# Three slots more between the first layer norm's sums and its mean, and one weight unit's low part moved to VectorE

## The chip, the cores and the metric

The kernel runs on one core of a Trainium2 chip. The metric is the device time of one launch in microseconds (us); lower is better. The engines are PE (TensorE, matrix products), ACT (ScalarE), DVE (VectorE), POOL (GpSimd) and SP (SyncE, which only issues DMAs). Each engine works through its own instruction queue in order.

## The reference, cut to what matters

Two layers of a trunk over 256 latent and 256 context tokens with 1024 channels. In each layer an input projection feeds a convolution branch, an attention branch and sigmoid gates:

```
u = a * sigmoid(g); u = dwconv1d(u, dw, dw_b)          # 31 taps, 512 channels
u = silu(layernorm(u, ln_g, ln_b))                     # mean and variance over the 512 channels
y_conv = u @ w_conv_out
y_attn = merge_heads(neighbourhood_attention(...)) @ w_na_out
x = x + g1 * ((sigmoid(gate0) * y_conv + sigmoid(gate1) * y_attn) @ w_out)
```

A gated feed-forward network follows. The modulation vectors (shift, scale and gate of each norm) are products of a conditioning vector with a 1024 x 6144 matrix per layer.

## The kernel before, in words

Every weight product is made of three: a weight tile is split into a high part and a low part, and so is the activation, and `mm3` issues high x high (L187), weight high x activation low (L188) and weight low x activation high (L189). Weights come in units of 128 x 1024 (512 KB), each loaded by SP into one of four buffers `raw`. ACT rounds a unit to its high part `whi` (four buffers). The low part `wlo` (four buffers) is made in one of two ways. `wunit` has DVE subtract: `whi` by L168 on ACT, `wlo` by L169 on DVE. `wadded` is for the units listed in `ADDED`: ACT makes `whi` by L206, then its negative by L207 into `wlo`, and POOL issues a DMA that adds `raw` onto it (L208). A `raw` buffer is free for the next unit only when L169 has read it or the L208 transfer has landed; a `whi` buffer only when the last product that reads it is done.

Work that is not a weight product runs as generators in a list `side`. `slot()` advances each generator to its next `yield`. `group` calls it twice in each 24 products of a 512-wide gate tile, and once more often where a group has only 12 products (the branch projections). So the slots pace the side work against PE.

Two generators matter here. `ada_dots` makes the modulation vectors: it loads a unit of `w_ada` (buffers `own`) and DVE takes its dot product with one or two vectors (L293, two instructions of 128 x 1024 a unit, each followed by a short read of the accumulator). `layer_norm` first finishes the convolution taps (L659), then adds the four channel tiles (L940 to L942 into `ss`), and has PE multiply the sum by ones, which takes the mean over channels and copies it to all partitions (L945, into the PSUM bank `po`). DVE subtracts it (L948), ACT squares (L333, L340), DVE adds the squares (L344), some slots later PE sums them over channels (L358), DVE and POOL take the root (L366, L368), PE spreads it (L374), and L956 to L960 scale, apply swish and split the result into `sh` and `sl`.

The place is the first layer's gate tiles: U_IN+14+n is the unit of gate n. After the gates comes the attention branch's projection (units U_NA to U_NA+3, 8 groups of 12 products, read `oh` and `ol`; DVE multiplies each group with its gate by L983), then `finish(ln)`, then the convolution branch's projection (units U_CO on, reads `sh`, `sl`).

Program order alone does not set an engine's queue: the tile framework schedules the recorded instructions, so a shift of a generator by a slot reorders neighbours on several engines.

Of the kernel before, what the change touches and what calls it, by code (L numbers as in the profile page):

```python
# [43 lines left out]

U_GLU0, U_V, U_IN, U_NA, U_CO, U_WO, U_UP, U_DN = 0, 2, 6, 36, 40, 44, 52, 96
NU = 118
ADDED = {*((0, U_IN + i) for i in (*range(19), 20, 22, 24, 26, 28)), *((0, u) for u in (U_NA + 1, U_NA + 3, *range(U_CO, U_CO + 4))), *((1, U_IN + i) for i in (7, 8, 9, 14, 15, 16, 17))}
T_GLU, T_Q, T_K, T_GATE = 0, 6, 10, 14

SWAP16 = [(i + 16) % 32 for i in range(32)]  # L50
# [3 lines left out]
def trunk(ctx: ExitStack, tc: tile.TileContext, xt, cvec, crow, wall, wada, params, bias_t, rope_t, out):  # L54
# [13 lines left out]
    def nm(s):  # L68
        uid[0] += 1
        return f"{s}_{uid[0]}"  # L70
# [3 lines left out]
    def psum(tag="main"):  # L74
        return psp.tile([P, 512], F32, tag=tag, bufs=BANKS[tag], name=nm(tag))

    def tmp(w=512):
        return tp.tile([P, w], F32, tag="t", bufs=5, name=nm("t"))
# [68 lines left out]
    def pr(l, off, n):  # L147
        return par[:, l * NPAR + off : l * NPAR + off + n]
# [29 lines left out]
    def wunit(l, u, at=None, cuts=1):  # L178
        w, more = wparts(l, u, at, cuts)
        more()  # L180
        return w

    def cols(w, i):
        return sl(w[0], i), sl(w[1], i)
# [16 lines left out]
    def wadded(l, u):  # L201

        r = raw_unit(wall[l, u])
        hi = wp.tile([P, UW], F32R, tag="whi", bufs=4, name=nm("whi"))
        lo = wp.tile([P, UW], F32R, tag="wlo", bufs=4, name=nm("wlo"))
        act.copy(hi, r)  # L206
        act.mul(lo, hi.bitcast(F32), -1.0)  # L207
        pool.dma_start(lo, r, accum_op=ALU.add)  # L208
        return hi, lo

    def unit8(l, u, at=None):
        w = wadded(l, u) if (l, u) in ADDED else wunit(l, u, at)
        return [cols(w, i) for i in range(KD)]
# [133 lines left out]
    def sum_squares(n, T, apart=False):  # L347

        at = tp.tile([P, 512], F32, tag="ss", name=nm("ss"))
        return [SumSq(T, at[:, i * T : (i + 1) * T], apart) for i in range(n)]  # L350

    def rstd(ss, n, bank, rest=0):

        nt = ss.T // P
        pt = psum("pt")
        for i, p in enumerate(ss.parts):
            for t in range(nt):
                pe.matmul(  # L358
                    pt[:, t : t + 1], sl(p, t), one, start=i == 0 and t == 0, stop=i == len(ss.parts) - 1,
                    skip_group_check=True,  # L360
                )
        return (yield from root(pt, nt, n, bank, rest))
# [255 lines left out]
    for l in range(DEPTH):  # L618
        last = l == DEPTH - 1
# [4 lines left out]
        with ExitStack() if last else start as e1a:  # L624
# [21 lines left out]
            def conv_tap(j, t):  # L646
                if after[0] is not None:
                    with tc.issue_after(after[0].ins):
                        tap(j, t)
                else:  # L650
                    tap(j, t)
# [264 lines left out]
            with ExitStack() as e1c:  # L916
# [12 lines left out]
                def layer_norm():  # L929

                    while taps:
                        for _ in range(6 if last else 5):
                            if taps:
                                conv_tap(*taps.pop(0))
                        yield
                    pace[0] = 1.0 if last else 1.1
                    flat = [c.rearrange("p s t -> p (s t)") for c in cb]
                    sm = tp.tile([P, 512], F32, tag="ss", name=nm("ss"))
                    eng = pool if last else dve
                    eng.tensor_tensor(sm[:, :T], flat[0], flat[1], ALU.add)  # L940
                    eng.tensor_tensor(sm[:, :T], sm[:, :T], flat[2], ALU.add)
                    dve.tensor_tensor(sm[:, :T], sm[:, :T], flat[3], ALU.add)  # L942
                    yield
                    pm = psum("po")
                    pe.matmul(pm[:, :T], one.to_broadcast([P, P]), sm[:, :T], start=True, stop=True)  # L945
                    (s2,) = sum_squares(1, T)
                    for j in range(KC):
                        dve.scalar_tensor_tensor(flat[j], pm[:, :T], -1.0 / CONV, flat[j], ALU.mult, ALU.add)  # L948
                        s2.add(flat[j], j == KC - 1)
                    for _ in range(2 if last else 5):  # L950
                        yield
                    pb = yield from rstd(s2, CONV, "po", 0 if last else 2)
                    for j in range(KC):
                        sg = tmp()
                        g, b = pr(l, LNG + j, 1), pr(l, LNB + j, 1)
                        dve.scalar_tensor_tensor(flat[j], flat[j], g, pb[:, :T], ALU.mult, ALU.mult)  # L956
                        act.activation(sg[:, :T], flat[j], AF.Sigmoid, bias=b)
                        dve.scalar_tensor_tensor(flat[j], flat[j], b, sg[:, :T], ALU.add, ALU.mult)
                        act.copy(sh_[j], flat[j])
                        dve.tensor_tensor(sl_[j], flat[j], sh_[j].bitcast(F32), ALU.subtract)  # L960
                        yield
                    if last:
                        pace[0] = 0.4

                side.remove(conv)
                ln = layer_norm()
                add_side(ln)
                for n in range(n, 2 * KD):
# [5 lines left out]
                def branch(base, xh, xl):  # L974
                    for n in range(0, KD, 2):
                        w = (wadded if (l, base + n // 2) in ADDED else wunit)(l, base + n // 2)
                        for i in range(2):
# [68 lines left out]
        with ExitStack() as e2:  # L1046
# [45 lines left out]
            if last:  # L1092
# [14 lines left out]
                for i, ps in enumerate(pss):  # L1107
                    b = small([P, 1], "wb", 4)
                    act.copy(b, ps[:, S : S + 1])
                    u = ef.tile([P, S], F32, name=f"u{l}_{i}")  # L1110
# [221 lines left out]
```

## Time and profile before

| | |
|---|---|
| median of 3 runs | 1118.74 us (1118.72 to 1119.91) |
| the profiled execution's own time | 1120.4 us |
| its span, first to last instruction | 1118.6 us |
| PE busy | 1097.3 us, 98% of the span |
| DVE busy | 897.0 us, 80% |
| ACT busy | 591.1 us, 53% |
| POOL busy | 45.9 us, 4% |
| mean granted TensorE clock | 0.995 of full speed |

PE is busy nearly all the time, so a change is worth what it does to the few gaps in PE's row; an idle gap on another engine counts only if PE waits for what comes after it. The views used are the page, the waits (who waited for whom), the timeline (instructions in order of time with start, duration, engine, line, tile and in brackets the idle time before it) and the windows (busy time and granted clock in chosen stretches).

### The profile page before, as it was taken

The numbers are of one execution on the slowest core, as the hardware profiler recorded it, in microseconds if no ns is written. First come the engines' busy times: TensorE is split into PE (matmuls) and PEld (weight loads), VectorE is DVE, ScalarE is ACT, GpSimd is POOL, SyncE is SP. The second block draws the span as 40 slices with busy tenths as digits, with TensorE's granted clock in tenths as the row PEclk, the third lists the DMA queues.
The fourth block names the chain that finished last, engine by engine and source line by source line (L and its number), as shares of the span: only waits on it lengthen the run. The fifth ranks groups of instructions, "written<-read, shape, count | busy, mean of one in ns | idle before, by whom it ended". The sixth has DMA issues, their size and how long they took to land.

```text
span 1118.6 us, 18099 instructions
## 1 busy us (share of the span) xinstructions
PE 1097.3 (98%) x6900; PEld 952.0 (85%) x6900; DVE 897.0 (80%) x1634; ACT 591.1 (53%) x974; POOL 45.9 (4%) x61
## 2 busy tenths in 40 slices
PE   8999999899999999999999999999999999999997
PEld 7677777678889988888888888989889999999997
DVE  5568898889898788888888555789799888988773
ACT  4458878445333543434343223544877657666642
POOL 1011110010000000000000000000100000000000
PEclk9999999999999999999999999999999999999999
DMA  9978663967953354554557656557863574665781
GB/s 362 288 198 223 154 165 86 280 184 217 284 164 94 112 153 151 169 170 150 170 170 215 219 186 190 181 196 196 226 187 138 151 259 156 191 196 179 222 268 57
DMA packets 60806, 211.35 MB, mean 189 GB/s; under 512 B 7344, under 2 KB 7600, under 8 KB 60720
## 3 DMA queue, kind: packets, MB, share of 16 engines
q1 hardware_dynamic: 55104, 190.77, 53.1%
q0 software_dynamic: 5328, 19.40, 9.1%
q8 instruction: 54, 0.88, 0.3%
q14 instruction: 32, 0.26, 0.1%
q10 hardware_dynamic: 288, 0.04, 0.0%
HBM read 187.63 MB, written 1.05 MB: 169 GB/s over the span
## 4 chain that ended last, share of the span: by engine, by line
PE 77%; issue 7%; DVE 6%; ACT 5%; DMA 3%; SPq 1%; POOL 0%; POOLq 0%; DVEq 0%; ACTq 0%
PE main L187 23%; PE main L189 23%; PE main L188 23%; PE main L729 4%; DVE cb L659 3%; SPq L721 1%; DMA raw<-in_wall 1%; DMA sb<-in_crow 1%; PE sc L189 1%; PE sc L188 1%; DMA wlo<-raw 1%; PE sc L187 1%; ACT whi L206 1%; ACT wlo L207 1%; DVE wlo L169 1%
## 5 line engine op out<-in xcount | busy, mean ns | idle before, releaser
L187 PE MATMUL main<-h,whi 128*128 128x256 f32 (+1 forms) x1328 | 446.8, 337 | 0.0
L189 PE MATMUL main<-h,wlo 128*128 128x256 f32 (+1 forms) x1328 | 444.0, 336 | 2.6 <-DMA wlo<-raw 1.6
L188 PE MATMUL main<-h,whi 128*128 128x256 f32 (+1 forms) x1328 | 442.6, 334 | 0.1
L168 ACT CAST whi<-raw 128x1024 fp32r<-128x1024 f32 (+1 forms) x207 | 213.9, 1037 | 235.9 <-DMA raw<-in_wall 115.5
L169 DVE TENSOR_TENSOR wlo<-raw,whi 128x1024 fp32r<-128x1024 f32 (+1 forms) x207 | 248.3, 1206 | 91.2 <-ACT whi L168 90.3
L189 PEld LDWEIGHTS main<-h,wlo 128*128 128x128 f32 x1328 | 249.7, 189 | 32.1 <-DMA wlo<-raw 1.8
L187 PEld LDWEIGHTS main<-h,whi 128*128 128x128 f32 x1328 | 249.7, 188 | 30.7 <-issue 2.2
L188 PEld LDWEIGHTS main<-h,whi 128*128 128x128 f32 x1328 | 250.1, 189 | 28.4 <-DVE h L390 0.5
L659 DVE SCALAR_TENSOR_TENSOR cb<-u,par,cb 128x512 f32<-128x512 f32 (+1 forms) x240 | 144.3, 616 | 3.0
L187 PE MATMUL main<-fh,whi 128*128 128x256 f32 (+1 forms) x386 | 123.0, 319 | 0.0
L188 PE MATMUL main<-fl,whi 128*128 128x256 f32 (+1 forms) x386 | 122.9, 318 | 0.0
L189 PE MATMUL main<-fh,wlo 128*128 128x256 f32 (+1 forms) x386 | 122.9, 318 | 0.0
L293 DVE CUSTOM_DVE_ANT_0 t<-raw,sb,par 128x1024 bf16<-128x1024 f32 x72 | 91.5, 1278 | 0.0
L189 PEld LDWEIGHTS main<-fh,wlo 128*128 128x128 f32 x386 | 72.7, 188 | 5.6
L188 PEld LDWEIGHTS main<-fl,whi 128*128 128x128 f32 x386 | 72.7, 188 | 5.6
L187 PEld LDWEIGHTS main<-fh,whi 128*128 128x128 f32 x386 | 72.7, 188 | 5.5
L1059 ACT ACTIVATE t<-main,par 128x512 f32<-128x512 f32 (+1 forms) x82 | 50.7, 669 | 39.2 <-PE main L189 39.2
L206 ACT CAST whi<-raw 128x1024 fp32r<-128x1024 f32 x37 | 38.9, 1052 | 47.2 <-PE main L188 24.5
L293 DVE CUSTOM_DVE_ANT_0 t<-own,sb,par 128x1024 bf16<-128x1024 f32 x48 | 60.1, 1279 | 3.9 <-ACT g L704 3.9
L1060 DVE SCALAR_TENSOR_TENSOR t<-main,par,t 128x510 f32<-128x510 f32 (+1 forms) x82 | 47.6, 615 | 10.6 <-ACT t L1059 10.3
L1063 DVE SCALAR_TENSOR_TENSOR t<-main,par,t 128x510 f32<-128x510 f32 (+1 forms) x82 | 46.6, 610 | 0.0
L389 ACT ACTIVATE h<-t,mod 128x256 fp32r<-128x256 f32 x56 | 25.5, 502 | 37.8 <-DVE t L388 37.8
(222 smaller groups left out, 1295.1 us busy)
## 6 DMA issues: line engine op xcount, KB each, us to landing
raw<-in_wall SPq DMA_DIRECT2D x239, 512.0 KB, 4.4
raw<-in_wada SPq DMA_DIRECT2D x64, 512.0 KB, 4.5
wlo<-raw POOLq DMA_DIRECT2D x37, 512.0 KB, 6.2
own<-in_wada SPq DMA_DIRECT2D x24, 512.0 KB, 4.9
bias<-in_bias_t SPq DMA_DIRECT2D x8, 520.0 KB, 5.0
row<-in_wada SPq DMA_DIRECT2D x8, 512.0 KB, 4.8
sb<-in_crow SPq DMA_DIRECT2D x5, 512.0 KB, 5.9
x<-in_xt SPq DMA_DIRECT2D x8, 256.0 KB, 4.4
```

The lines of the kernel that those rows point to most:

```text
L168: act.copy(hi[:, c], r[:, c])
L169: dve.tensor_tensor(lo[:, c], r[:, c], hi[:, c].bitcast(F32), ALU.subtract)
L187: pe.matmul(ps, w[0], xh, start=start, stop=False)
L188: pe.matmul(ps, w[0], xl, start=False, stop=False)
L189: pe.matmul(ps, w[1], xh, start=False, stop=stop)
L206: act.copy(hi, r)
L293: dve.tensor_tensor_reduce(tmp().bitcast(BF16), r, v, 1.0, pr(l, BADA + n, 1), ALU.mult, ALU.add, mods[l][:, n, s : s + 1])
L659: dve.scalar_tensor_tensor(cb[j], src, w, cb[j], ALU.mult, ALU.add)
L729: mm = pe.matmul(pv[t], h1[n == 1][k][:, c], w[n == 2][:, b], start=k + n == 0, stop=k == KD - 1 and n == 2)
L1059: act.activation(c, pv_, AF.Identity, bias=pr(l, FDB + t, 1), scale=w[1])
L1060: dve.scalar_tensor_tensor(c[:, :, 1:], pv_[:, :, : S - 1], w[0], c[:, :, 1:], ALU.mult, ALU.add)
L1063: dve.scalar_tensor_tensor(c[:, :, : S - 1], pv_[:, :, 1:], w[2], c[:, :, : S - 1], ALU.mult, ALU.add)
```

## The change

In the first layer, `layer_norm` yields four times instead of once between the last addition into `ss` (L942) and the product that takes the mean, so that this product and all that follows it in the generator is recorded three slots later. In the second layer the unit U_IN+17, the weights of gate 3, leaves `ADDED`: its low part comes from a subtraction on DVE (L169) and no longer from ACT's L207 and POOL's accumulating DMA L208. All lines after L943 have a number greater by one in the changed kernel.

```diff
-ADDED = {..., *((1, U_IN + i) for i in (7, 8, 9, 14, 15, 16, 17))}
+ADDED = {..., *((1, U_IN + i) for i in (7, 8, 9, 14, 15, 16))}
 ...
                     dve.tensor_tensor(sm[:, :T], sm[:, :T], flat[3], ALU.add)
-                    yield
+                    for _ in range(1 if last else 4):
+                        yield
                     pm = psum("po")
                     pe.matmul(pm[:, :T], one.to_broadcast([P, P]), sm[:, :T], start=True, stop=True)
```

Three places show how the queues move. In the rows a name's number says which buffer's use it is.

On DVE, in the first layer, from the dot products on the unit own_2197 to the sum `ss` and the mean's subtraction. Before:

```order
L293 ISA t_2293,mod_108<-own_2197,sb_2165,par 128x1024
L293 ISA mod_108 128x1
L659 SCALAR_TENSOR_TENSOR cb_3_202<-u_3_215,par,cb_3_202 128x512
L169 TENSOR_TENSOR wlo_2375<-raw_2373,whi_2374 128x1024
L659 SCALAR_TENSOR_TENSOR cb_3_202<-u_3_215,par,cb_3_202 128x512 x3
L169 TENSOR_TENSOR wlo_2469<-raw_2467,whi_2468 128x1024
L659 SCALAR_TENSOR_TENSOR cb_3_202<-u_3_215,par,cb_3_202 128x512 x3
L942 TENSOR_TENSOR ss_2297<-ss_2297,cb_3_202 128x512
```

And now, from the low part wlo_2358 on:

```order
L169 TENSOR_TENSOR wlo_2358<-raw_2356,whi_2357 128x1024
L659 SCALAR_TENSOR_TENSOR cb_3_202<-u_3_215,par,cb_3_202 128x512
L293 ISA t_2374,mod_108<-own_2295,sb_2162,par 128x1024
L293 ISA mod_108 128x1
L659 SCALAR_TENSOR_TENSOR cb_3_202<-u_3_215,par,cb_3_202 128x512
L293 ISA t_2376,mod_108<-own_2295,sb_2165,par 128x1024
L293 ISA mod_108 128x1
L659 SCALAR_TENSOR_TENSOR cb_3_202<-u_3_215,par,cb_3_202 128x512
L169 TENSOR_TENSOR wlo_2460<-raw_2458,whi_2459 128x1024
L659 SCALAR_TENSOR_TENSOR cb_3_202<-u_3_215,par,cb_3_202 128x512
L942 TENSOR_TENSOR ss_2297<-ss_2297,cb_3_202 128x512
```

Between the tap after own_2197 and these rows the changed queue also has the two dots of own_2247, each with a tap behind it. So four dots that stood behind L942 now stand ahead of it, and two of them ahead of the low part wlo_2358 (wlo_2375 before), which the next gate tile reads. On PE the mean's product stood behind 23 products of the gate tile main_2332; now it stands behind all 24 of the same tile (main_2315) and 18 of the next one (main_2355), 19 products later.

On PE, at the attention branch's projection: main_2775 is the last group of U_NA+1, main_2801 and main_2821 read U_NA+2 (whi_2796, wlo_2797), main_2842 and main_2862 read U_NA+3 (whi_2837, wlo_2838). Before, the groups followed one another; now:

```order
L189 MATMUL main_2775<-oh_3_206,wlo_2751 128x512
L187 MATMUL main_2801<-oh_0_203,whi_2796 128x512
L188 MATMUL main_2801<-ol_0_207,whi_2796 128x512
L187 MATMUL main_2821<-oh_0_203,whi_2796 128x512
L188 MATMUL main_2821<-ol_0_207,whi_2796 128x512
L187 MATMUL main_2842<-oh_0_203,whi_2837 128x512
L188 MATMUL main_2842<-ol_0_207,whi_2837 128x512
L187 MATMUL main_2862<-oh_0_203,whi_2837 128x512
L188 MATMUL main_2862<-ol_0_207,whi_2837 128x512
L189 MATMUL main_2801<-oh_0_203,wlo_2797 128x512
```

Two products of each of the four groups, those that read only the high parts, come first; ten of each follow, group by group. On DVE the low part wlo_2797 (L169) moves from ahead of the gate product of main_2755 (L983) to behind that of main_2775.

On ACT at the same place, with U_CO's units whi_2884 and whi_2927. Before:

```order
L206 CAST whi_2837<-raw_2835 128x1024
L704 ACTIVATE g_15_2690<-main_2653 128x512
L206 CAST whi_2884<-raw_2882 128x1024
L207 ACTIVATE wlo_2838<-whi_2837 128x1024
L207 ACTIVATE wlo_2885<-whi_2884 128x1024
L206 CAST whi_2927<-raw_2925 128x1024
```

And now:

```order
L206 CAST whi_2837<-raw_2835 128x1024
L704 ACTIVATE g_15_2690<-main_2647 128x512
L960 CAST sh_3_2171<-cb_3_202 128x512
L206 CAST whi_2884<-raw_2882 128x1024
L206 CAST whi_2927<-raw_2925 128x1024
L207 ACTIVATE wlo_2838<-whi_2837 128x1024
```

The negative that starts U_NA+3's low part now stands behind the rounding of U_CO+1's unit.

More of the change, by code (lines that the diff above doesn't have):

```diff
@@ L46 @@
 NU = 118
-ADDED = {*((0, U_IN + i) for i in (*range(19), 20, 22, 24, 26, 28)), *((0, u) for u in (U_NA + 1, U_NA + 3, *range(U_CO, U_CO + 4))), *((1, U_IN + i) for i in (7, 8, 9, 14, 15, 16, 17))}
+ADDED = {*((0, U_IN + i) for i in (*range(19), 20, 22, 24, 26, 28)), *((0, u) for u in (U_NA + 1, U_NA + 3, *range(U_CO, U_CO + 4))), *((1, U_IN + i) for i in (7, 8, 9, 14, 15, 16))}
 T_GLU, T_Q, T_K, T_GATE = 0, 6, 10, 14
```

## The prediction

> **What bounds the kernel now.** I read the page first.
>
> ```profile
> span 1118.6 us, 18099 instructions
> PE 1097.3 (98%) x6900; PEld 952.0 (85%) x6900; DVE 897.0 (80%) x1634; ACT 591.1 (53%) x974; POOL 45.9 (4%) x61
> ```
>
> PE is without work for 21 us in all, so the change can win only from its waits and can lose by making new ones. Next, PE's waits: engine, tile and line, what was waited for, then us in total, times, longest.
>
> ```profile
> PE po L945 <- DVE ss L942: 4.9, 1, 4.9
> PE main L189 <- DMA wlo<-raw: 1.6, 1, 1.6
> ```
>
> The first is the wait the first edit stands at. The timeline of PE there (start, us, engine, line):
>
> ```profile
> 218.18 0.40 PE L188 MATMUL main<-h,whi 128*128 128x512 f32 x1
> 223.50 2.04 PE L945 MATMUL po<-ss,one 128*128 128x512 f32 x2 [4.93 <-DVE ss L942]
> 225.77 0.63 PE L187 MATMUL main<-h,whi 128*128 128x512 f32 x1
> 227.83 0.40 PE L189 MATMUL main<-h,wlo 128*128 128x512 f32 x1
> 234.81 0.40 PE L189 MATMUL main<-h,wlo 128*128 128x512 f32 x1
> ```
>
> 218.18 is product 23 of main_2332; after the wait comes the mean's product, then product 24, and at 227.83 product 30. From there 30 products take 6.98 us, 0.233 each. The windows (stretch, PE busy, ..., granted clock, DMA share, GB/s) show a second cost behind the wait:
>
> ```profile
> 220.00:220.50 0.50, 0.00 (x0) 0.00 (x0) 0.50 (x2) 0.00 (x0) 0.00 (x0) 1.00 1.01 385
> 220.50:221.00 0.50, 0.00 (x0) 0.00 (x0) 0.50 (x1) 0.00 (x0) 0.00 (x0) 0.90 0.87 328
> 227.50:228.00 0.50, 0.50 (x3) 0.46 (x2) 0.50 (x1) 0.50 (x3) 0.04 (x1) 0.77 0.00 0
> 813.00:813.60 0.60, 0.00 (x0) 0.00 (x0) 0.60 (x3) 0.60 (x3) 0.00 (x0) 1.00 1.12 232
> ```
>
> The clock falls to half at 220.9, 2.3 us after PE's last product ended (218.18 + 0.40), and is back at about 227.7. In the shorter wait of the second layer, 1.6 us, it holds.
>
> What does the mean's product cost at full clock? The second layer's is half as wide:
>
> ```profile
> 872.26 0.60 PE L945 MATMUL po<-ss,one 128*128 128x256 f32 x2
> 872.81 0.28 PE L188 MATMUL main<-ol,whi 128*128 128x256 f32 x1
> ```
>
> From 872.26 to 872.81 there is one other product, 0.12 us, which leaves 0.43, so 0.86 for 512 columns. Before, 0.86 + 6 x 0.233 = 2.26 us of work took 227.83 - 223.50 = 4.33: the half clock cost 2.07.
>
> **Part one: when the sum is ready.** DVE, not PE, sets this. Its timeline before:
>
> ```profile
> 212.06 1.28 DVE L293 CUSTOM_DVE_ANT_0 t<-own,sb,par 128x1024 bf16<-128x1024 f32 x1
> 213.26 0.75 DVE L659 SCALAR_TENSOR_TENSOR cb<-u,par,cb 128x512 f32<-128x512 f32 x1
> 213.93 1.29 DVE L293 CUSTOM_DVE_ANT_0 t<-own,sb,par 128x1024 bf16<-128x1024 f32 x1
> 215.79 1.23 DVE L169 TENSOR_TENSOR wlo<-raw,whi 128x1024 fp32r<-128x1024 f32 x1
> 216.93 2.33 DVE L659 SCALAR_TENSOR_TENSOR cb<-u,par,cb 128x512 f32<-128x512 f32 x3
> 222.66 0.69 DVE L942 TENSOR_TENSOR ss<-ss,cb 128x512 f32<-128x512 f32 x1
> ```
>
> There is no gap in it. By start to start a dot takes 1.20, a tap after a dot 0.67, a low part 1.14, a tap after a tap 0.78. At 215.79 the queues part. The changed one has four dots (4.8), two low parts (2.3) and six taps, five at 0.67 and one at 0.78 (4.1), before L942: 11.2 us, so it starts at 227.0 instead of 222.66. PE started 0.84 after L942 before (222.66 to 223.50), so the mean's product starts at 227.8. The sum is 4.3 later and the product stands 19 places later, 19 x 0.233 = 4.4 us. The wait is not taken away; it moves with its product.
>
> It is cut in two, though. wlo_2358 follows two dots and two taps: 215.79 + 3.74 = 219.53, done at 220.76, and PE can go on at 220.9. PE wants it for product 27, due at 218.18 + 4 x 0.233 = 219.1: a wait of 1.8. Then products 27 to 42, 16 x 0.233, to 224.6, and a wait of 3.2 for the sum until 227.8. Together 5.0, against 4.9 now.
>
> What is won is the place: at 227.8 PE has 42 products behind it. With the clock held, product 43 starts at 227.8 + 0.86 = 228.7; before it starts at 227.83 + 13 x 0.233 = 230.9. That is -2.2. If the clock falls in the 3.2 us, I price one spell as 3.4 us at half rate, half of the 6.8 us for which it was down before: +1.7, leaving -0.5. No row shows a wait of this length. 3.2 lies beyond the 2.3 us after which the clock did fall, and 1.6 us left it; I take -0.5, ends -2.2 and -0.1 (the old 2.07 again).
>
> The Trainium skill, TensorE: Matmul & The Clock Gate, section HAM oscillation, states as a rule that only PE gaps above about 3.4 us bring the clock down. By that both waits would pass unpunished and this term would be -2.2; the row that drops at 2.3 us speaks against leaning on it.
>
> **Part two: the attention projection.** Moving dots and the mean's chain also reorders ACT and DVE here. Let E be the end of main_2775. PE before (the first of the 96 products of this projection, the first of main_2801, the first L189 of main_2842, and the product after the 96th), then DVE, ACT and POOL beside them:
>
> ```profile
> 267.07 0.40 PE L187 MATMUL main<-oh,whi 128*128 128x512 f32 x1
> 278.07 0.39 PE L187 MATMUL main<-oh,whi 128*128 128x512 f32 x1
> 284.02 0.39 PE L189 MATMUL main<-oh,wlo 128*128 128x512 f32 x1
> 289.06 0.39 PE L187 MATMUL main<-sh,whi 128*128 128x512 f32 x1
> 278.27 0.69 DVE L983 TENSOR_TENSOR g<-main,g 128x512 f32<-128x512 f32 x1 [0.29 <-PE main L189]
> 278.04 1.05 ACT L206 CAST whi<-raw 128x1024 fp32r<-128x1024 f32 x1 [2.21 <-PE main L188]
> 279.12 1.06 ACT L207 ACTIVATE wlo<-whi 128x1024 fp32r<-128x1024 f32 x1
> 275.28 1.83 POOL L208 DMA_DIRECT2D wlo<-raw  x2 [10.02 <-ACT wlo L207]
> 280.58 0.87 POOL L208 DMA_DIRECT2D wlo<-raw  x1 [3.48 <-ACT wlo L207]
> ```
>
> A product takes (289.06 - 267.07) / 96 = 0.229 here, and E was 278.07. The L206 at 278.04 is whi_2927, which waits for the last L188 of main_2775. In the changed queue it stands ahead of wlo_2838's L207. So that L207, which led to POOL's issue at 275.28 (E - 2.8), now cannot start before whi_2927 is done; the rows 278.04, 279.12 and 280.58 are just such a chain and put POOL's issue at E + 2.5.
>
> PE meanwhile does the eight high products, 8 x 0.229 = 1.83. wlo_2797 comes after the gate product of main_2775: start E + 0.20, 0.61 to the next start, 1.22 for L169, 0.15 to PE: E + 2.18, a wait of 0.35 (ends 0 and 1.6, one more dot of 1.2 ahead). Then 20 products, and the first L189 on wlo_2838 is due at E + 6.76.
>
> When does it land? Rows of the transfers: those issued at 264.40, 275.28 and 280.58 in that order (us from issue to landing last), and all 37.
>
> ```profile
> wlo<-raw POOLq DMA_DIRECT2D x1, 512.0 KB, 6.8
> wlo<-raw POOLq DMA_DIRECT2D x1, 512.0 KB, 7.9
> wlo<-raw POOLq DMA_DIRECT2D x1, 512.0 KB, 9.7
> DMA to landing us min/median/max: 4.4/6.2/10.9
> ```
>
> Before, 275.28 + 7.9 = 283.2 was ahead of the L189 at 284.02, by 0.8. After, the wait is 2.5 + landing - 6.76, that is landing less 4.2: 0.2 at the fastest, 6.7 at the slowest. I take 7.4, between the two units of this same projection: +3.2. Two more such transfers follow at once, and loads of raw and own run beside them, which keeps me off the median.
>
> The Trainium skill, DMA: Bandwidth & Descriptors, section Anatomy of one DMA, fits such a POOL transfer as 2.0 us plus bytes over 436e3, an estimate of 3.2 us for 512 KB. By that there would be no wait and the sum below would be -0.75; the fastest of 37 rows, 4.4, already lies above it.
>
> The remaining reordered steps have cover. DVE idles before L957 until PE's L374, but `sh` and `sl` are wanted only after 289. The dots need `own` loads that SP issues well ahead. Without that cover each 1.2 us dot in front of a gate product would count.
>
> **Part three: gate 3 of the second layer.** POOL and PE before:
>
> ```profile
> 805.76 0.87 POOL L208 DMA_DIRECT2D wlo<-raw  x1 [1.47 <-ACT wlo L207]
> 810.06 0.86 POOL L208 DMA_DIRECT2D wlo<-raw  x1 [3.42 <-ACT qk L869]
> 813.61 0.38 PE L189 MATMUL main<-h,wlo 128*128 128x256 f32 x1 [1.58 <-DMA wlo<-raw]
> ```
>
> The removed transfer is the one at 810.06. PE waits for the one at 805.76 (the third query unit), which lands at 813.6 and shares its last 3.5 us with it. Its start does not move. Alone it may land earlier, by at most the 1.58 waited; I take 0.6 off, a landing of 7.2 for 7.8. ACT loses a L207 (1.06) and DVE gains a L169 (1.2) ahead of a softmax; the mean's sum there has PE idle nowhere, so DVE's share is hidden. If it were not, it costs up to 0.5. Ends -1.6 and +0.5.
>
> **The sum**, against the median (the profiled execution, 1120.4, is its span plus 1.8 and lies 1.7 above the median, which I put on both sides): -0.5 + 0.35 + 3.2 - 0.6 = +2.45, so 1121.2. All ends together, with one more clock drop (2.1) in the second wait, give -3.6 and +10.8.
>
> **Rivals.** A measurement can tell about 0.2%, 2.2 us, from no change.
>
> - Forecast, 0.45: wlo_2838 becomes the new wait and the clock falls at the sum. Own range 1119.8 to 1123.5; 0.08 of it within the bound.
> - The clock holds, 0.27: -2.2 for -0.5 gives +0.75, 1119.5; with the median landing of 6.2 also, 1118.3. For it: 1.8 and 3.2 are apart by 3.7 us of products. Against: the 2.3.
> - Faster, 0.15: accumulating transfers land quickly where fewer run together. It decides at a landing of 4.5 us: wlo_2838 then costs 0.2, the query unit's wait goes (-1.6), and with the clock held -2.2 + 0.35 + 0.2 - 1.6 = -3.25, 1115.5. For it: the minimum of 4.4. Against: the rows of this stage quoted above are 6.8 and more.
> - Much slower, 0.13: landing 9.7 (+5.5), and the clock falls in that wait as well (+2.1): +6.85, 1125.6.
>
> That the edit does not remove the wait it stands at is part of the forecast.
>
> **The numbers.** The likeliest case gives 1121.2. The range 1116.6 to 1124.6 leaves out most of the fast case (0.12) and the slower half of the last (0.08). Faster 0.15; within 0.27 + 0.08 = 0.35; slower 0.37 + 0.13 = 0.50.
>
> **What would show it.** PE's waits should list L946 for ss at 3.2 and an L189 for a DVE low part at 1.8 just ahead, then a L189 for a DMA of about 3 in the main<-oh groups, and the query unit's 1.6 shorter. The clock row should dip once near 228. I am wrong if the wait for ss is under 1.5, if no L189 on `oh` waits for a transfer, or if waits appear after `sh`.

## The result, and the profile after

The changed kernel takes 1121.74 us (median of 21 runs, 1119.76 to 1126.9) against 1119.6 us (21 runs of before, 1118.34 to 1122.03). The ratio is 1.0022 with a 95% interval of 1.0013 to 1.0031: slower by about 2.5 us. The forecast was 1121.2 us, slower. The profiled execution took 1120.83 us, its span 1119.0 us.

PE's waits in the changed kernel (line, what was waited for, us in total, times, longest):

```profile
PE po L946 <- DVE ss L942: 3.0, 1, 3.0
PE main L189 <- DVE wlo L169: 2.9, 3, 1.7
PE main L189 <- DMA wlo<-raw: 2.4, 1, 2.4
```

The one wait of 4.9 has become two, 1.7 and 3.0, and a transfer is waited for that was in time before. Where they stand on PE's timeline, and below it the two on DVE's that they wait for (start, us; the number in brackets is the wait ahead):

```profile
217.96 0.39 PE L188 MATMUL main<-h,whi 128*128 128x512 f32 x1
220.07 0.50 PE L189 MATMUL main<-h,wlo 128*128 128x512 f32 x1 [1.72 <-DVE wlo L169]
227.09 1.61 PE L946 MATMUL po<-ss,one 128*128 128x512 f32 x2 [3.03 <-DVE ss L942]
...
286.24 0.50 PE L189 MATMUL main<-oh,wlo 128*128 128x512 f32 x1 [2.45 <-DMA wlo<-raw]
290.94 0.39 PE L187 MATMUL main<-sh,whi 128*128 128x512 f32 x1
218.80 1.21 DVE L169 TENSOR_TENSOR wlo<-raw,whi 128x1024 fp32r<-128x1024 f32 x1
226.25 0.69 DVE L942 TENSOR_TENSOR ss<-ss,cb 128x512 f32<-128x512 f32 x1
```

217.96 is product 26 of the forecast's count, 220.07 product 27 on wlo_2358, 286.24 the first low product on wlo_2838, 290.94 the first product of the convolution branch. The windows (length of the stretch, then busy time of PE, weight loads, DVE, ACT and POOL, then granted clock, DMA share, GB/s) show one dip of the clock at the sum and none at the transfer:

```profile
227.00:227.50 0.50, 0.41 (x1) 0.30 (x2) 0.00 (x0) 0.00 (x0) 0.00 (x0) 1.00 1.15 238
227.50:228.00 0.50, 0.50 (x3) 0.34 (x1) 0.00 (x0) 0.00 (x0) 0.00 (x0) 0.54 0.95 229
230.50:231.00 0.50, 0.50 (x2) 0.36 (x2) 0.50 (x2) 0.14 (x1) 0.00 (x0) 0.55 1.10 311
231.00:231.50 0.50, 0.50 (x4) 0.40 (x3) 0.21 (x1) 0.50 (x1) 0.00 (x0) 1.00 0.83 246
286.00:287.00 1.00, 0.76 (x3) 0.67 (x4) 0.10 (x2) 0.00 (x0) 0.50 (x1) 1.00 1.05 274
```

Half rate lasts from 227.54 to 230.95, 3.4 us. And ACT and POOL at the attention projection (E, the end of main_2775, is 276.86 here):

```profile
276.87 1.05 ACT L206 CAST whi<-raw 128x1024 fp32r<-128x1024 f32 x1 [4.49 <-PE main L188]
277.83 2.95 ACT L207 ACTIVATE wlo<-whi 128x1024 fp32r<-128x1024 f32 x3
279.29 2.76 POOL L208 DMA_DIRECT2D wlo<-raw  x3 [21.27 <-DVE wlo L169]
```

ACT stands idle 4.49 us in front of whi_2927's rounding, and three negatives that need nothing from PE stand behind it. POOL's three transfers start together, the first at 279.29.

Which stretch pays? Times between landmarks of PE's timeline in the profiled executions: product 23 of main_2332 (the row ahead of the wait, less three pitches of 0.233 where that row is product 26), first product on `oh`, first on `sh`, first L374 after 300 us, the second layer's mean.

| kernel | 23 to oh | oh to sh | sh to L374 | L374 to second mean |
|---|---|---|---|---|
| before | 48.9 | 22.0 | 60.6 | 522.6 |
| changed | 48.6 | 25.1 | 61.2 | 520.8 |
| slots alone | 48.2 | 26.3 | 60.6 | 521.2 |
| unit alone | 49.8 | 22.6 | 60.6 | 521.5 |
| changed, negative first | 48.1 | 22.4 | 60.6 | 523.2 |
| five slots | 45.7 | 22.0 | 60.6 | 521.2 |
| six slots, negative first | 43.7 | 26.1 | 61.0 | 521.8 |
| seven slots | 43.7 | 22.0 | 60.6 | 524.7 |

The loss is in the second column. Moving the sum's wait (first column) is about neutral. Before and unit alone have the same queues there and differ by 0.9, and that is the clock: it was at half for 6.83 us in both, but from 220.90 in one and from 222.60 in the other, so 4.2 and 6.2 us of it fell on work behind the wait, and half of that is lost. With the waits and this half taken off, all eight first columns come to 41.8 to 42.2 us. In the last column taking off the wait for the third query unit's transfer (down the table 1.58, 0, 0, 0.45, 2.17, 0, 0 and 3.37 us) leaves 520.8 to 521.8 in all eight; the experiments show why that wait varies. The changed kernel's profiled span is only 0.4 above before's, since its last column happened to be 1.8 shorter; the medians say 2.1.

### The profile page after: what moved, and what is told of

Its sections match the earlier page's. It is cut to its first block, busy times and chain, and to the rows that moved or that the text cites. A ratio compares the mean times of both kernels' runs of the same rounds, so it can differ in the third digit from the quotient of the medians.

```text
span 1119.0 us, 18087 instructions
## 1 busy us (share of the span) xinstructions
PE 1097.6 (98%) x6900; PEld 951.6 (85%) x6900; DVE 897.5 (80%) x1635; ACT 589.6 (53%) x973; POOL 44.0 (4%) x60
## 4 chain that ended last, share of the span: by engine, by line
PE 75%; DVE 8%; issue 7%; ACT 4%; DMA 3%; SPq 1%; POOLq 0%; DVEq 0%; POOL 0%; ACTq 0%
PE main L187 22%; PE main L188 22%; PE main L189 22%; PE main L729 4%; DVE cb L659 3%; DMA raw<-in_wall 1%; DVE t L293 1%; SPq L721 1%; PE sc L187 1%; DMA sb<-in_crow 1%; PE sc L189 1%; PE sc L188 1%; PE po L220 1%; DVE wlo L169 1%; DMA wlo<-raw 1%
## 5 line engine op out<-in xcount | busy, mean ns | idle before, releaser
L168 ACT CAST whi<-raw 128x1024 fp32r<-128x1024 f32 (+1 forms) x208 | 214.8, 1037 | 231.7 <-DMA raw<-in_wall 109.3
L169 DVE TENSOR_TENSOR wlo<-raw,whi 128x1024 fp32r<-128x1024 f32 (+1 forms) x208 | 249.4, 1205 | 88.9 <-ACT whi L168 87.8
```

The source lines that it names most:

```text
L168: act.copy(hi[:, c], r[:, c])
L169: dve.tensor_tensor(lo[:, c], r[:, c], hi[:, c].bitcast(F32), ALU.subtract)
```

## The experiments

**The two edits apart.** First edit alone:

```diff
-ADDED = {..., *((1, U_IN + i) for i in (7, 8, 9, 14, 15, 16))}
+ADDED = {..., *((1, U_IN + i) for i in (7, 8, 9, 14, 15, 16, 17))}
```

> The first edit alone (four yields, U_IN+17 of the second layer still in ADDED). Theory A (the change is a loss in the first layer, partly paid back in the second): the wait for ss at L946 stays at about 3.0 us, the L189 on wlo_2358 waits about 1.7, an L189 of the attention projection waits 2 to 3 for its transfer, and the query unit's wait of 1.6 for a transfer is there again. Time: before + 2.1 + 1.5, about 3.6 us slower than before (between 2.5 and 4.5), so slower than the changed kernel by about 1.5. Rival B (the first edit moves its wait and costs nothing, the second edit's subtraction on DVE costs the time): within 1 us of before.

Measured: 1122.31 us against 1119.88, ratio 1.0022 (1.0007 to 1.0037), 2.4 slower where 2.5 to 4.5 was expected. The loss is the changed kernel's own, not 1.5 more, so rival B falls and the first edit carries the loss; but theory A's second half (the second edit pays back) is not borne out. In the profile no transfer is waited for at the query unit, though gate 3's transfer is there. At the projection:

```profile
220.58 0.50 PE L189 MATMUL main<-h,wlo 128*128 128x512 f32 x1 [1.38 <-DVE wlo L169]
227.60 1.21 PE L946 MATMUL po<-ss,one 128*128 128x512 f32 x2 [3.03 <-DVE ss L942]
286.33 0.68 PE L189 MATMUL main<-oh,wlo 128*128 128x512 f32 x1 [2.05 <-DMA wlo<-raw]
288.52 0.63 PE L188 MATMUL main<-ol,whi 128*128 128x512 f32 x1
288.95 0.63 PE L189 MATMUL main<-oh,wlo 128*128 128x512 f32 x1
```

The transfer's wait is 2.05, shorter than the changed kernel's 2.45, and yet the stretch is longer, 26.3 for 25.1: products behind it come at 0.43 instead of 0.23. The windows (columns as above) have the clock at half there from 286.5 to about 289.9:

```profile
286.00:286.50 0.50, 0.17 (x1) 0.17 (x2) 0.50 (x1) 0.21 (x1) 0.00 (x0) 0.98 0.98 254
286.50:287.00 0.50, 0.50 (x2) 0.41 (x3) 0.08 (x2) 0.00 (x0) 0.38 (x1) 0.50 1.05 270
289.00:290.00 1.00, 1.00 (x4) 0.81 (x3) 0.00 (x0) 0.00 (x0) 0.00 (x0) 0.55 1.10 246
```

Second edit alone:

```diff
-    ... (7, 8, 9, 14, 15, 16, 17))}
+    ... (7, 8, 9, 14, 15, 16))}
```

> The second edit alone (one yield as before, U_IN+17 of the second layer out of ADDED). Theory A: the wait of 4.9 for ss is as before, the query unit's wait of 1.6 falls to under 0.3, and the time is 1 to 1.6 us below before. Rival B: the subtraction of 1.2 us on DVE ahead of a softmax is waited for, and the time is 1 to 2 us above before.

Measured: 1120.16, ratio 1.0011 (1.0001 to 1.0021). Theory A's gain of 1 to 1.6 is excluded, and rival B's mechanism is not seen: no softmax step waits longer. PE's wait at the query unit is 0.45 in this profile. So the second edit gains nothing, and costs at most 2.4.

**The order on ACT.** The changed kernel, with U_CO+1's rounding queued behind U_NA+3's negative:

```diff
-        act.copy(hi, r)
-        act.mul(lo, hi.bitcast(F32), -1.0)
+        with tc.issue_after(negs[0, U_NA + 3].ins) if (l, u) == (0, U_CO + 1) else ExitStack(): act.copy(hi, r)
+        negs[l, u] = act.mul(lo, hi.bitcast(F32), -1.0)
```

> The changed kernel with one order forced on ACT: the rounding of U_CO+1's unit (whi_2927, L206) is queued behind the negative of U_NA+3's (wlo_2838, L207). Nothing else moves. Theory A (POOL's transfer of U_NA+3 is late only because its negative stands behind a rounding that waits for PE): POOL issues it 2 to 4 us ahead of main_2775's end instead of 2.4 behind it, the wait of 2.4 for wlo in the projection goes to under 0.3, and the time falls by 2.0 to 2.8 against the changed kernel, to within 0.8 us of before. Rival C (these transfers land late because several run together): the issue is earlier but a wait of 1 us or more for a transfer stays in the projection or appears ahead of the first product on sh, and the time falls by less than 1 us.

Measured: 1120.62, ratio 1.0005 (0.9989 to 1.0021). That is 0.7 above before, within the 0.8 expected, but only 1.1 us below the changed kernel's median, less than the 2.0 to 2.8 expected, in intervals that overlap. The profile shows the place itself plainly. ACT and POOL:

```profile
270.79 1.05 ACT L206 CAST whi<-raw 128x1024 fp32r<-128x1024 f32 x1 [3.45 <-PE main L188]
271.75 2.00 ACT L207 ACTIVATE wlo<-whi 128x1024 fp32r<-128x1024 f32 x2
276.28 1.05 ACT L206 CAST whi<-raw 128x1024 fp32r<-128x1024 f32 x1 [2.54 <-PE main L188]
273.20 1.83 POOL L208 DMA_DIRECT2D wlo<-raw  x2 [15.73 <-ACT wlo L207]
```

The negatives now run at 271.75, ahead of the rounding that waits for PE, and POOL issues 3.1 us ahead of E (276.31 here) instead of 2.4 behind it. No product on `oh` waits for a transfer, so rival C falls, and the second column falls from 25.1 to 22.4. Part of what this execution gains is lost at another transfer, in the second layer, which this edit does not touch:

```profile
812.79 0.39 PE L189 MATMUL main<-h,wlo 128*128 128x256 f32 x1 [2.17 <-DMA wlo<-raw]
```

**Who makes the sum late.** The changed kernel with the dots paced at 0.5 (lines 923 and 936):

```diff
-                    pace[0] = 1.1
+                    pace[0] = 0.5
 ...
-                    pace[0] = 1.0 if last else 1.1
+                    pace[0] = 1.0 if last else 0.5
```

> The changed kernel with the dot products of the first layer paced at 0.5 instead of 1.1 from the end of the attention until the attention projection, so that 4 of them and not 8 stand ahead of L942 on DVE (6 products fewer stand ahead of the mean's product). Theory A (DVE's dots carry the wait for ss): L942 starts about 4.5 us earlier than in the changed kernel, the product is due 1.4 + 1.7 earlier, the wait for ss falls from 3.0 to 1.0 to 2.0, no low part is waited for ahead of it, and the clock holds through it; with nothing new further on the time falls by 3 to 6 us against the changed kernel, to 1 to 4 below before. Rival D (a later stage pays): the dots that are put off stand ahead of gate products or of x's update in the output projection, waits for DVE appear there, and the time stays within 1.5 us of the changed kernel.

Measured: 1133.08, ratio 1.0118 (1.0102 to 1.0134). The sum's wait is 2.2, just above the 1.0 to 2.0 expected, and no low part is waited for ahead of it. L942 starts 13.6 us after the first dot (211.30 to 224.86), against 18.0 in the changed kernel (208.24 to 226.25): the dots do carry it. But a later stage pays, as rival D said, and by far more than the 1.5 us it allowed: the time is 11.3 above the changed kernel's. PE's waits:

```profile
PE po L374 <- POOL rs L368: 7.5, 2, 6.9
PE sc L189 <- DVE wlo L169: 6.0, 1, 6.0
PE po L946 <- DVE ss L942: 2.2, 1, 2.2
```

The dots that were put off stand in one block of thirteen on DVE, ahead of the step of the root (L366) that this L374 waits for, so the dots cannot simply be slowed. First and last of the block, and that step:

```profile
345.55 1.28 DVE L293 CUSTOM_DVE_ANT_0 t<-own,sb,par 128x1024 bf16<-128x1024 f32 x1
360.03 1.28 DVE L293 CUSTOM_DVE_ANT_0 t<-own,sb,par 128x1024 bf16<-128x1024 f32 x1
361.24 0.15 DVE L366 TENSOR_SCALAR red<-pt 128x2 f32<-128x2 f32 x1
```

**More slots.** One more than the change, with the second edit taken back:

```diff
-                    for _ in range(1 if last else 4):
+                    for _ in range(1 if last else 5):
```

> Five slots instead of four, with the second edit taken back. DVE's order up to L942 is that of the changed kernel, but the mean's product stands behind 24 products of the tile instead of 18, and the scheduler now puts wlo_2838's negative ahead of the roundings of U_CO's units. Theory A: L942 starts where it does in the changed kernel, so the wait for ss falls by 6 x 0.233 = 1.4, from 3.0 to 1.6, the low part ahead of it is still waited for by 1.3 to 1.7, and no transfer is waited for in the attention projection. With the clock dip (1.7) the first layer then gains about 2 against before, without it 3.7: 1.5 to 4 us below before. Rival E (slots cost time wherever they are put, since the chain behind the mean comes later): a new wait at the convolution branch's first products on sh, and the time is not below before.

Measured: 1114.51, ratio 0.9956 (0.9942 to 0.9969), 5 us below before, past the 1.5 to 4 expected. One slot turns the loss into a gain. Its timeline of PE at the sum:

```profile
220.56 0.50 PE L189 MATMUL main<-h,wlo 128*128 128x512 f32 x1 [1.80 <-DVE wlo L169]
227.57 1.10 PE L946 MATMUL po<-ss,one 128*128 128x512 f32 x2 [1.63 <-DVE ss L942]
```

And its windows:

```profile
226.00:227.00 1.00, 0.00 (x0) 0.00 (x0) 0.97 (x3) 1.00 (x2) 0.00 (x0) 1.00 1.11 287
228.00:229.00 1.00, 1.00 (x5) 0.59 (x4) 0.86 (x2) 0.00 (x0) 0.00 (x0) 1.00 1.01 320
230.00:231.00 1.00, 1.00 (x6) 0.82 (x5) 1.00 (x2) 1.00 (x3) 0.00 (x0) 1.00 0.77 311
```

The sum is as late as in the changed kernel, but the product stands six products (1.4 us) later, and the wait is 1.63 for 3.03. The clock holds at 1.00 throughout. In the first column that is 48.6 to 45.7, 2.9 us, of which 1.4 is the wait; the other 1.5 is close to the dip of 3.4 us at half rate (1.7) that is gone. And the scheduler, with that slot, puts U_NA+3's negative ahead of the other roundings by itself:

```profile
269.88 1.06 ACT L207 ACTIVATE wlo<-whi 128x1024 fp32r<-128x1024 f32 x1
274.29 1.05 ACT L206 CAST whi<-raw 128x1024 fp32r<-128x1024 f32 x1 [3.35 <-PE main L188]
271.34 0.88 POOL L208 DMA_DIRECT2D wlo<-raw  x1 [3.68 <-ACT wlo L207]
```

No transfer is waited for at the projection and the second column is 22.0 again. 2.9 + 3.1 is 6.0 of the 7.2 us between the two medians.

Six slots (`range(1 if last else 6)`), with the order on ACT forced as above:

> Six slots, the negative of U_NA+3 forced ahead of U_CO+1's rounding on ACT, the second edit taken back. The mean's product stands 18 products later than in the changed kernel, and DVE has one dot pair more and one low part less ahead of L942 (1.3 us more). Theory A: the wait for ss is 3.0 + 1.3 - 4.2, nothing (under 0.4); only the low part's wait of 1.3 to 1.7 is left, the clock holds, no transfer is waited for in the projection: 4 to 6 us below before. Rival E: sh comes too late, PE waits for ACT or DVE before its first products on sh by 1 us or more, and the gain is under 2 us. Rival F (the clock dips all the same): about 3.5 below before with the clock at half for 3.4 us near 228.

Measured: 1118.71, ratio 0.9996 (0.9981 to 1.001): no gain that can be told from none, where 4 to 6 was expected. At the sum it went as theory A said: no wait, no dip, first column 43.7. Rival E named the right engine but not the place: PE waits 1.96 for DVE in the attention projection, ahead of the branch, with the clock at half after it, and the second column is 26.1.

```profile
275.46 0.75 PE L187 MATMUL main<-oh,whi 128*128 128x512 f32 x1 [1.96 <-DVE g L984]
```

As in the changed kernel the high products of four groups come first, so all four `main` banks are wanted at once, and the gate product L984 that frees one stands behind dots on DVE.

Five slots, and two low parts taken off DVE:

```diff
-ADDED = {*((0, U_IN + i) for i in (*range(19), 20, 22, 24, 26, 28)), ...}
+ADDED = {*((0, U_IN + i) for i in (*range(19), 20, 21, 22, 23, 24, 26, 28)), ...}
```

> Five slots, and the low parts of units 21 and 23 of the first layer's input by ACT and POOL's transfer instead of DVE; the second edit taken back. DVE has two low parts less ahead of L942 (2 us). Theory A: no low part is waited for ahead of the mean (its 1.4 gone), and the wait for ss is about 1.3 (1.6 + 1.4 - 2.0 and the rest); clock held; 3 to 6 us below before. Rival G (transfers pay): with seven units in a row by POOL, wlo lands late and L189 waits 1 us or more for a transfer in a gate tile, and the time is within 1.5 us of before or above.

Measured: 1117.35, ratio 0.9979 (0.9962 to 0.9997), 2.8 above five slots alone. The low part's wait is gone, but the sum's is 3.19, not 1.3, and the clock dips. L942 starts no earlier than with five slots (226.62 for 226.74): the first dot started 1.7 later (210.40 for 208.72), when the unit that it reads had landed, which took back what DVE saved behind it. So the low part's wait moved to the sum. Why that load was late here is not shown, and the profiled execution (1120.79) lies 3.4 above this run's median.

```profile
210.40 1.28 DVE L293 CUSTOM_DVE_ANT_0 t<-own,sb,par 128x1024 bf16<-128x1024 f32 x1 [5.71 <-DMA own<-in_wada]
227.46 2.04 PE L946 MATMUL po<-ss,one 128*128 128x512 f32 x2 [3.19 <-DVE ss L942]
```

Seven slots (`range(1 if last else 7)`), nothing else:

> Seven slots, the second edit taken back, nothing forced on ACT (the scheduler puts wlo_2838's negative ahead of the next rounding by itself). The mean's product stands 30 products later than in the changed kernel. Theory A: no wait for ss; the low part wlo_2358 is waited for by 1.3 to 1.7; wlo_2460, now behind L942 and two dots, by 0 to 0.5; the time is 3.5 to 6 us below before. Rival E: the chain behind the mean ends 2.5 us or more later than with five slots and the first products on sh wait for it: less gain than six slots by 1 us or more.

Measured: 1114.63, ratio 0.9955 (0.994 to 0.9969). No wait for the sum, 1.68 for the low part, none at `sh`: rival E falls. It does not beat five slots, though its first column is 2.0 shorter; its profile waits 3.37 us for the query unit, and five slots' waits nothing there. What its other executions waited there is not known.

**The idle stretch on DVE.** In before too DVE stands idle ahead of the first dot, with taps behind it in its queue that need nothing:

```profile
200.39 4.68 DVE L659 SCALAR_TENSOR_TENSOR cb<-u,par,cb 128x512 f32<-128x512 f32 x6
208.98 1.29 DVE L293 CUSTOM_DVE_ANT_0 t<-own,sb,par 128x1024 bf16<-128x1024 f32 x1 [3.91 <-ACT g L704]
```

The bracket names ACT's L704, but the dot reads `own`: SP issued its unit at 197.47 and it landed 11.4 us later, at 208.9 (11.6 with five slots, 13.2 with low parts off DVE). So the first dots were held behind the taps recorded by then and started two steps of their pace later (`lasttap` is the tap recorded last; `left` starts at -2), first in the kernel before:

```diff
-                dve.tensor_tensor_reduce(
+                with tc.issue_after(lasttap[0].ins) if early and not i else ExitStack(): dve.tensor_tensor_reduce(
 ...
-                    g1 = ada_dots(0, range(16, 40), sb0, own, 2)
+                    g1 = ada_dots(0, range(16, 40), sb0, own, 2, -2)
```

> The kernel before, one slot, both edits taken back; only the first two dot products of the first layer (unit own_2195) are held behind the convolution taps recorded by then and start two steps of their pace later. In before, DVE stands idle 3.9 us ahead of the first dot (until 208.98), which waits for its operands, while taps that need nothing are queued behind it. Theory A2 (that idle stretch, not the place of the mean's product, makes the sum late): DVE has no gap of over 1 us there, L942 starts at about 216 instead of 222.7, the mean's product, now behind 14 products fewer, waits about 1.2 instead of 4.9, the clock holds: 4 to 7 us below before. Rival H (the dots are only put off, as with slower dots): they are late for the norm of the second half, PE waits there as at 362 in the run with slower dots, and the time is within 1 us of before or above.

Measured: 1116.2, ratio 0.9964 (0.9948 to 0.9981), about 4 us below before, and rival H falls: no wait at the second half's norm. But theory A2 holds only in part. L942 starts at 217.35, 5.3 earlier than in before, yet PE still waits 4.04 for it, not 1.2, and the clock falls there for 6.83 us:

```profile
209.99 1.22 DVE L169 TENSOR_TENSOR wlo<-raw,whi 128x1024 fp32r<-128x1024 f32 x1 [2.92 <-DMA own<-in_wada]
217.35 0.69 DVE L942 TENSOR_TENSOR ss<-ss,cb 128x512 f32<-128x512 f32 x1
218.19 2.04 PE L945 MATMUL po<-ss,one 128*128 128x512 f32 x2 [4.04 <-DVE ss L942]
206.05 1.06 ACT L273 ACTIVATE sb<-sb 128x1024 f32<-128x1024 f32 x1 [3.40 <-DMA sb<-in_crow]
208.91 1.04 ACT L168 CAST whi<-raw 128x1024 fp32r<-128x1024 f32 x1
```

Of the idle stretch 2.92 is left, now ahead of a low part. The bracket names a load of `own`, which L169 does not read; the `whi` that it reads was done by ACT's L168 at 209.95, and L168 stood in ACT's queue behind L273, which waited 3.40 for a load. The scheduler also placed the mean's product 14 products earlier, which takes 3.3 of the 5.3 back. The profiled execution was the slowest of its twelve (1122.95): it waits 2.90 for the query unit's transfer and has a second dip of 3.41 behind that wait. So how the median gains 4 us is not settled by it.

The same with five slots (`range(1 if last else 5)`):

> The same hold of the first dots, with five slots. The mean's product stands behind 39 products more than with one slot and the same hold, DVE's queue up to L942 is the same. Theory A2: no wait for ss and none for a low part ahead of it, no clock dip, no transfer waited for in the attention projection: 1 to 2 us below the one-slot version with the hold, 6 to 8 below before, and 1 to 3 below five slots without the hold. Rival H: dots late for the norm of the second half; not below five slots without the hold.

Measured: 1114.68 (six runs, 1110.77 to 1117.63), ratio 0.9943 (0.9924 to 0.9963). Neither the sum nor a low part is waited for in the first layer, as A2 said. The gain over before is 5.5, not 6 to 8, and against five slots without the hold there is none that can be measured. Its profiled execution, the slowest of the six, waits 3.31 for the query unit, with a dip of 3.41 behind it.

**The query unit's transfer.** The kernel before, with that unit's low part by DVE and gate 3's left as it was:

```diff
-    ... (7, 8, 9, 14, 15, 16, 17))}
+    ... (7, 8, 14, 15, 16, 17))}
```

> The kernel before, but the third query unit of the second layer (U_IN+9) leaves ADDED, so DVE makes its low part; gate 3 stays in. Theory J (PE's wait there, 0 to 3.4 us from run to run, is the time this one transfer takes less 6.3, whether gate 3's transfer runs beside it or not): no L189 waits for a transfer near 812, the median falls by 1 to 2 us against before and the spread of the runs is narrower than before's. Rival K (it was gate 3's transfer that delayed it, or DVE's subtraction comes late among the softmax's steps): a wait of 0.5 us or more for a low part or for a softmax step takes its place, and the time is within 0.5 us of before.

Measured: 1120.27, ratio 1.0003 (0.9994 to 1.0013). No transfer is waited for there, and the runs lie closer together (12 from 1119.11 to 1122.32, for 23 of before from 1118.05 to 1126.05), both as theory J said, but the time is before's. A softmax step now waits, as rival K said:

```profile
824.35 0.45 PE L480 MATMUL pt<-qk,qk 64*128 64x416 f32 x1 [1.30 <-ACT pT L549]
```

That ACT step (823.82) stands behind ACT's L869 (823.54), which waits 2.03 for DVE's L848, and DVE has two low parts (819.33 and 821.20) ahead of that.

## Why the prediction was right

- **The sum's wait moves with its product.** Confirmed, to two tenths: 1.72 and 3.03 measured for 1.8 and 3.2, L942 at 226.25 for 227.0 (the whole stretch ran 0.9 earlier; the cause lies upstream and is open).
- **One dip of the clock, half of the old one.** Confirmed: one dip of 3.4 us. The first term came to -0.3 in the changed kernel and -0.7 and -0.8 in the two runs with the same queues here, for -0.5: -0.4 from the dip (1.7 for 2.1 lost), -0.2 to -0.6 from the waits, and 0.3 unexplained the other way. The rival in which the clock holds lost in all three. That is in part luck: the prediction went by the wait's length alone, but behind the query unit's wait the clock fell at 3.31 us and held at 3.37 (last section). The Trainium skill's rule for the clock (TensorE: Matmul & The Clock Gate, HAM oscillation), only gaps above about 3.4 us, would have made the term -2.2; these traces disagree with it, with dips at waits of 3.0 and of 2.05.
- **The attention projection.** The mechanism is shown: POOL's issue came at E + 2.4 for E + 2.5, the landing took 6.9 us for 7.4, the wait was 2.45 for 3.2, and it vanished when the negative alone was put first. With wlo_2797's 0.25 (0.35 forecast) the place cost 2.7 of wait, 3.1 in the landmark table. Without the second dip it is under the 3.55 forecast, and with it (slots alone) over it, 4.3. The margin of 0.8 that before had here is not safe either: unit alone, taps first and query unit by DVE, which keep one slot, waited 0.37, 0.43 and 0.63 for a transfer here. The estimate of 3.2 us from the Trainium skill's DMA: Bandwidth & Descriptors, Anatomy of one DMA, would have left no wait; the transfer took more than twice that.
- **Gate 3 of the second layer.** Here the step failed, though its size was inside the ends given. It forecast -0.6 from less sharing. The edit alone gave 1.0011, and the query unit's wait does not follow it: with gate 3's transfer it was 1.58, 0, 0, 0, 3.29, 3.37, 2.90 and 3.31 us in eight profiles, without it 0, 0.45, 2.17 and 0. POOL issues the query unit's transfer 6.0 to 6.3 us before it is due wherever there is a wait, so the wait is the landing less that lead, and the landing differs from run to run.
- **The sum.** -0.3 + 0.25 + 2.45, and the rest of the projection's 3.1, is about 2.8; forecast without the last term 3.05. The medians rose 2.1 and the ratio says 2.5. That the forecast of 2.45 came so near is luck to the extent that two errors cancel: the projection cost less than 3.55 (2.7 of wait), and gate 3 did not win its 0.6. A wait of 0.3 for L992 appeared far behind `sh` (at 318.28) in the changed kernel alone; the prediction had named waits there as a sign of being wrong, and none was forecast.

## What to carry to other kernels

A slot between a producer and its consumer moves work on every engine that the slots pace; count what it pulls ahead of the producer before counting what it gives the consumer, and try the neighbouring counts, since here four slots lost 2.5 us and five won 5. Look for the instruction that waits at the head of an in-order queue with ready work behind it: that was the loss on ACT, and on DVE holding that instruction back brought the sum 5.3 us earlier. A wait that is a transfer's time less a fixed lead is not removed by an edit that leaves the lead as it is; compare several profiles before crediting an edit with its absence.

## What the runs showed of the hardware that was not expected

- A wait's length alone does not decide whether the clock falls; where the wait lies counts too. Within one execution the clock changes only on a grid of 3.413 us. With taps first and five slots it changed at 103.68, 107.09, 810.23 and 813.65, and 810.23 - 103.68 is 207.0 steps; with slots alone it fell at 228.45 and 286.48, 17.0 steps apart. The same holds in every trace with more than one dip, and the place of the grid differs from one trace to the next. So a dip lasts 3.41 us or a multiple of it: 6.83 in before, 17.06 with slower dots at 360 (the last dip of each trace is cut off by its end).
- Between 200 and 1100 us, in the thirteen traces, the clock fell after every step of the grid at full clock in which PE had stood idle for 1.96 us or more (15 falls), and held after every step with 1.88 or less. Two waits of nearly the same length, both for the query unit, show it (columns as above). The first two rows are the steps of the wait of 3.37 with seven slots, 1.88 and 1.50 idle; the grid there is counted back from the clock's only fall, at 1109.33. The others are the step of the wait of 3.31 with taps first and five slots, 2.75 idle, and the step behind it:

```profile
805.54:808.96 3.42, 1.54 (x14) 1.34 (x12) 3.38 (x14) 3.42 (x10) 0.41 (x1) 1.00 1.04 259
808.96:812.37 3.41, 1.91 (x16) 1.92 (x17) 2.06 (x5) 2.24 (x5) 0.00 (x0) 1.00 1.06 247
806.83:810.24 3.41, 0.66 (x5) 0.67 (x6) 3.30 (x10) 3.41 (x10) 0.00 (x0) 1.00 1.05 279
810.24:813.65 3.41, 3.41 (x18) 3.41 (x17) 0.31 (x1) 0.42 (x1) 0.00 (x0) 0.50 1.04 331
```

In the changed kernel the step that ends at 227.54 has 2.96 idle, the one that ends at 285.57 has 1.78, and the clock fell at the first only. Before 200 us it fell twice after less (1.80 and 1.15 idle), so idle time is not the whole rule. A wait of 2 to 3.4 us should be priced both with and without the 1.7 us of a dip.

- The same transfer of 512 KB, issued at the same lead, landed in under 6.3 us in some executions and in 9.7 in others (issued at 800.79, waited for until 810.46, with seven slots). That alone moves a run by up to 3.4 us, more than the whole effect of this change, and by 1.7 more where the clock falls behind the wait.
